# An output projection by seven block products instead of eight, for half of the tokens of a hybrid attention layer

## The chip, the cores and the metric

The kernel runs on one core of one Trainium2 chip. The metric is the device time of one execution in microseconds (us). The engines are named as the profile names them: PE multiplies matrices and PEld loads its stationary operand, DVE, ACT and POOL work on vectors, and SP issues the transfers (DMA).

## The reference

One layer of a post-norm trunk, for 1024 tokens of 1024 dimensions, in float32. The part that changes is the product with `w_out`; its result goes into the first LayerNorm.

```python
h = x @ w_in                                   # q, k, v of two kinds of attention, and two gates
y_a = chunk_band_attention(...) @ w_proj_a     # 512 x 1024 weights
y_b = stick_breaking_attention(...) @ w_proj_b
mix = (sigmoid(ga + b) * y_a + sigmoid(gb + b) * y_b) @ w_out     # 1024 x 1024 weights
x = layer_norm(2 ** 0.25 * x + mix, ln1_g, ln1_b)
g, u = split(x @ w_ffn_in, 2)                  # 1024 x 5632
x = layer_norm(2 ** 0.25 * x + (silu(g) * u) @ w_ffn_out, ln2_g, ln2_b)
```

## The kernel before

**Arithmetic.** Every operand of a matrix product is split into a high part (a cast to fp32r on ACT) and a low part (operand minus high part, by a subtraction on DVE or POOL); `split` (L109) does it. One product of two 128-row operands is then three matmuls, high by high, high by low and low by high (`mm3`, L113), each 128x128 stationary by 128x512 moving, accumulated in one PSUM bank of 512 columns.

**Seven products.** The input projection, the v projection and most of the feed-forward layer already multiply 2x2 blocks by seven block products instead of eight (a Strassen-Winograd scheme). Sums of blocks of both operands are made on DVE, split, and seven products are accumulated in two banks per output block, which are read out between the products (`pair_steps` L185, `v_steps` L446, `down_seven` L1332). The product with `w_out` is a plain one.

**Stages, in order of the text.** (1) Input projection, 14 work items one after another (`run_pairs` L508). Each item's seven products take their turn on PE while ACT and DVE read the banks into tiles `c`, split them into `hi` and `lo` and SP stores them. Beside them the weights `w_proj` are split and stored for later, one block per item from the sixth step on (`store_proj` L558, called in `aside_work` L502). (2) Attention with gates and the first branch's projection woven in. (3) The second branch's projection (loop at L1024): for each of eight blocks `c` of 128 dimensions, in the order 6, 7, 5, 4, 0, 1, 2, 3, 24 matmuls fill two banks `yBps` of 512 tokens each (two banks in turn, tag `sc`). DVE multiplies each by the gate `gB` (L1042) and adds the other branch, `gA` or `mA` (L1043); the sum, transposed `mix`, is split into `mh[c]`, `ml[c]` (L1044). (4) Output projection (L1228): first over blocks 0 to 3 for all eight token tiles, then over blocks 4 to 7. Each of the 2 x 8 x 2 groups is 12 matmuls into a bank `ops`, which DVE adds to `acc_t[tt]`, loaded with `x` (L1244). In the second round a LayerNorm follows per token tile (`layer_norm` L1056), the result is stored, and at token tile 4 the transposes that make the feed-forward layer's operands begin (`x1_operands` L1079). (5) The feed-forward layer.

**Memory.** SBUF is cut into slots of 128 x 1024 float32 with fixed counts per tag (`SLOTS` L44): `bw` 9, `pt` 4, `yt` 3, `gt` 3, `kp` 4, `op` 8, `xt` 16, and `qs`, `kh`, `kl`, `v` with 2 each. `cycle(QKV, ...)` (L69) hands out these last four tags in turn. A tile waits until a slot of its tag is free, that is, until the last reader of an earlier tile is done. The three `gt` slots hold the raw weights of `w_out` before they are split.

**Order.** The text is unrolled. The order on each engine is not the order of the text: when the program is built, a planner replays it with its own costs, and gives each queue a fixed order in which, of what is ready, the earlier in the text goes first. SP's queue is one such order, and a transfer that waits for its slot holds up those queued behind it. `keep_in_program_order` pins single instructions.

**Weights of `w_out`.** `begin_w` (L537) issues the load into a raw slot and returns `end`, which splits it: a cast on ACT (L546) and a subtraction on the engine that is passed in (L547), here DVE.

Of the kernel before, what the change touches and what calls it, by code (L numbers as in the profile page):

```python
# [12 lines left out]
F32R = mybir.dt.float32r  # L13
# [5 lines left out]
P = 128  # L19
# [11 lines left out]
HW = 512  # L31
# [17 lines left out]
def hybrid_trunk_kernel(ctx: ExitStack, tc, x, xt, w_first, w_v, w_in, b_gate, rel_bias, w_proj,  # L49
# [452 lines left out]
    def aside_work(i):  # L502
        if i == 2:
            small_inputs()
        if i >= len(work) - 9:
            store_proj(i - len(work) + 9)

# [45 lines left out]
    def load_w(*args):  # L553
        return begin_w(*args)()

# [461 lines left out]
    mh, ml = [], []  # L1017
    for c in range(8):
        m_slot = of("bw") if c < 4 else lambda name, dtype: cycle(QKV, name, dtype)
        mh.append(m_slot(f"mh{c}", F32R))  # L1020
        ml.append(m_slot(f"ml{c}", F32R))
    acc_t = [slot(tag, f"acc{tt}") for tt, tag in enumerate(["pt"] * 4 + ["yt"] * 3 + ["bw"])]
    wo_ends, wo = [], []
    for n, c in enumerate((6, 7, 5, 4, 0, 1, 2, 3)):  # L1024
# [12 lines left out]
        for hf, cs in enumerate((LO, HI)):  # L1037
# [6 lines left out]
            split(mh[c][:, cs], ml[c][:, cs], mA[:, cs])  # L1044
        if wo_ends:
            wo.append(wo_ends.pop()(True))
        if 2 < n < 7:
            wo_ends.append(begin_w(w_out[(n - 3) * P:(n - 2) * P, :], f"o0_{n - 3}", of("gt"),
                                   of("xt"), nc.vector))
# [80 lines left out]
    for tt in range(8):  # L1130
        dma(acc_t[tt], x[tt * P:(tt + 1) * P, :])
# [96 lines left out]
    for half_k in range(2):  # L1228
        if half_k == 1:
            wo = [load_w(w_out[(4 + j) * P:(5 + j) * P, :], f"o1_{j}", of("gt"), of("xt"),  # L1230
                         nc.vector) for j in range(4)]
            left_f(0)
            R0 = slot("gt", "wRf0")
            dma(R0, w_ffn_in[NF])
            Wf[0]["hr"] = split_w(R0, "wrf0", "bw")
            left_f(1)
            right_f(1)
        for tt in range(8):
            ts_ = slice(tt * P, (tt + 1) * P)
            for hf, cs in enumerate((LO, HI)):  # L1240
                acc = bank("mm" if hf == 0 else "sc", f"ops{half_k}_{tt}_{hf}")
                mm3(acc, [(mh[4 * half_k + j][:, ts_], ml[4 * half_k + j][:, ts_],
                           wo[j][0][:, cs], wo[j][1][:, cs]) for j in range(4)])
                nc.vector.scalar_tensor_tensor(  # L1244
                    acc_t[tt][:, cs], acc_t[tt][:, cs], ALPHA if half_k == 0 else 1.0, acc,
                    ALU.mult, ALU.add)
            if half_k == 1:
# [4 lines left out]
                if tt == 3:  # L1252
                    left_f(2)
# [179 lines left out]
```

## Time and profile before

| | us |
|---|---|
| median of 3 runs (lowest to highest) | 1430.65 (1429.98 to 1431.88) |
| the profiled execution's own time | 1430.51 |
| its span, first to last instruction | 1428.7 |

The granted clock of PE in the profiled execution is 0.998 of full speed. The second branch's projection lies at 641 to 685 us of the span and the output projection at 685 to 777 us; the input projection ends at 333 us. In a row of the timeline the first number is the start, the second the duration, and a bracket tells how long the engine was idle before and who ended that. In the rows of stretches each engine has its busy time and, in brackets, its instructions.

### The profile page before, as it was taken

The numbers are of one execution on the slowest core, as the hardware profiler recorded it, in microseconds if no ns is written. First come the engines' busy times: TensorE is split into PE (matmuls) and PEld (weight loads), VectorE is DVE, ScalarE is ACT, GpSimd is POOL, SyncE is SP. The second block draws the span as 40 slices with busy tenths as digits, with TensorE's granted clock in tenths as the row PEclk, the third lists the DMA queues.
The fourth block names the chain that finished last, engine by engine and source line by source line (L and its number), as shares of the span: only waits on it lengthen the run. The fifth ranks groups of instructions, "written<-read, shape, count | busy, mean of one in ns | idle before, by whom it ended". The sixth has DMA issues, their size and how long they took to land.

```text
span 1428.7 us, 19071 instructions
## 1 busy us (share of the span) xinstructions
PE 1417.4 (99%) x6696; PEld 1177.0 (82%) x6696; DVE 1027.6 (72%) x1638; ACT 672.7 (47%) x1171; POOL 267.8 (19%) x317
## 2 busy tenths in 40 slices
PE   9999999999999999999999999999999999999997
PEld 7888888888888888888888888888888888888886
DVE  8857756645778778877768947776776756978757
ACT  6434444555778887863213634443444433212201
POOL 0000000003556788740023000000000000100016
PEclk9999999999999999999999999999999999999999
DMA  7475567858786579848412124443444458797602
GB/s 251 131 235 166 191 226 216 293 189 220 212 219 187 161 212 288 262 153 309 157 45 89 62 87 150 150 157 134 148 161 162 153 187 279 281 310 238 202 15 103
DMA packets 102544, 263.99 MB, mean 185 GB/s; under 512 B 11040, under 2 KB 27424, under 8 KB 102448
## 3 DMA queue, kind: packets, MB, share of 16 engines
q1 hardware_dynamic: 102448, 262.77, 56.7%
q8 instruction: 53, 0.87, 0.3%
q14 instruction: 43, 0.35, 0.1%
HBM read 170.94 MB, written 88.11 MB: 181 GB/s over the span
## 4 chain that ended last, share of the span: by engine, by line
PE 94%; DVE 3%; ACT 1%; DMA 1%; POOL 0%; issue 0%; POOLq 0%; SPq 0%; DVEq 0%; ACTq 0%
PE sxf L180 16%; PE sxp L180 8%; PE szf L180 8%; PE dx L1356 6%; PE v L483 5%; PE gps L579 4%; PE syf L180 4%; PE szp L180 4%; PE dz L1356 3%; PE yAps L876 3%; PE syp L180 2%; PE tp_b L787 2%; PE tp_a L787 2%; PE ops L118 2%; PE ops L117 2%; PE ops L120 2%
## 5 line engine op out<-in xcount | busy, mean ns | idle before, releaser
L1312 POOL TENSOR_TENSOR wdyt<-wdyt 128x512 f32<-128x512 f32 x8 | 11.2, 1394 | 512.3 <-ACT h L1184 422.6
L764 POOL TENSOR_TENSOR w_b<-w_b,kp_b 128x511 f32<-128x511 f32 (+3 forms) x96 | 96.1, 1011 | 31.1 <-DVE kp_b L759 21.8
L759 DVE TENSOR_TENSOR_SCAN kp_b<-kp_b,ident_ps 128x512 f32<-128x512 f32 (+2 forms) x64 | 56.6, 885 | 23.6 <-ACT kp_b L756 22.7
L756 ACT ACTIVATE kp_b<-sc_b 128x512 f32<-128x512 f32 (+3 forms) x96 | 48.4, 504 | 30.7 <-PE sc_b L676 25.0
L1064 POOL TENSOR_TENSOR mv<-mv,neghalf 128x1 f32<-128x1 f32 x16 | 23.9, 1494 | 207.7 <-DVE mv L1063 207.6
L699 POOL MEMSET bias<- 64x64 f32 x2 | 0.3, 144 | 313.7 <-ACT bias L695 313.7
L180 PE MATMUL szf<-x1S63h,wcf 128*128 128x512 f32 x168 | 55.1, 389 | 0.0
L111 DVE TENSOR_TENSOR pt_b<-tp_b,pt_b 128x512 fp32r<-128x512 f32 (+1 forms) x96 | 50.0, 544 | 6.6 <-ACT pt_b L110 5.9
L729 POOL TENSOR_SCALAR w_a<-w_a,st_a 128x640 f32<-128x640 f32 (+2 forms) x64 | 42.5, 668 | 60.5 <-PE sc_a L676 24.9
L1287 DVE TENSOR_TENSOR x<-dx,x 128x512 f32<-128x512 f32 x64 | 43.3, 686 | 14.6 <-PE dx L1356 14.6
L111 DVE TENSOR_TENSOR sl<-h,sl 128x512 fp32r<-128x512 f32 x56 | 38.4, 686 | 21.0 <-ACT sl L110 21.0
L110 ACT CAST sl<-h 128x512 fp32r<-128x512 f32 x56 | 34.7, 619 | 37.5 <-PE syf L180 17.1
L110 ACT CAST pt_b<-tp_b 128x512 fp32r<-128x512 f32 (+1 forms) x96 | 47.5, 505 | 8.0 <-PE tp_b L787 7.6
L118 PE MATMUL ops<-wl_o,mh 128*128 128x512 f32 x128 | 50.1, 392 | 0.0
L724 ACT ACTIVATE w_a<-w_a,st_a 128x640 f32<-128x640 f32 (+2 forms) x64 | 44.8, 701 | 11.1 <-DVE st_a L718 9.9
L120 PE MATMUL ops<-wh_o,ml 128*128 128x512 f32 x128 | 49.9, 390 | 0.0
L117 PE MATMUL ops<-wh_o,mh 128*128 128x512 f32 x128 | 49.7, 391 | 0.0
L1184 ACT ACTIVATE h<-sxf 128x512 f32<-128x512 f32 x21 | 12.5, 598 | 77.9 <-PE sxf L180 77.9
L111 DVE TENSOR_TENSOR pt_a<-tp_a,pt_a 128x512 fp32r<-128x512 f32 (+1 forms) x96 | 44.8, 485 | 5.6 <-ACT pt_a L110 4.0
L757 ACT ACTIVATE w_b<-sc_b 128x511 f32<-128x511 f32 (+3 forms) x96 | 48.6, 506 | 0.0
L787 PE MATMUL tp_b<-ident,w_b 128*128 128x128 f32 x288 | 47.8, 273 | 0.4 <-DVE pt_b L111 0.3
L110 ACT CAST pt_a<-tp_a 128x512 fp32r<-128x512 f32 (+1 forms) x96 | 39.2, 433 | 12.4 <-PE tp_a L787 11.6
(1740 smaller groups left out, 4778.6 us busy)
## 6 DMA issues: line engine op xcount, KB each, us to landing
s_dr<-sl SPq DMA_DIRECT2D x112, 256.0 KB, 2.3
sd<-s_dr SPq DMA_DIRECT2D x56, 512.0 KB, 4.6
wLf<-in_w_ffn_in_dram SPq DMA_DIRECT2D x22, 512.0 KB, 4.4
wRf<-in_w_ffn_in_dram SPq DMA_DIRECT2D x22, 512.0 KB, 3.7
v_dr<-vc SPq DMA_DIRECT2D x16, 512.0 KB, 3.0
qs<-q_dr SPq DMA_DIRECT2D x16, 512.0 KB, 5.7
kh<-k_dr SPq DMA_DIRECT2D x32, 256.0 KB, 5.8
kl<-k_dr SPq DMA_DIRECT2D x32, 256.0 KB, 5.6
```

The lines of the kernel that those rows point to most:

```text
L110: return (nc.scalar.copy(dst_h, src), nc.vector.tensor_tensor(dst_l, src, dst_h.bitcast(F32), ALU.subtract))
L111: nc.vector.tensor_tensor(dst_l, src, dst_h.bitcast(F32), ALU.subtract))
L117: mm(acc, lh, rh, start=(i == 0), stop=False)
L118: mm(acc, lh, rl, start=False, stop=False)
L120: mm(acc, ll, rh, start=False, stop=(i == n))
L180: mm(acc, lw[:, ks], rx, start=(first and kt == i == 0), stop=(kt == 3 and i == 2), skip_group_check=not first)
L483: mm(accs[j], a, b, start=(first and kt == n == 0), stop=(kt == 3 and n == 2), skip_group_check=True)
L579: mm(acc[hf], lw[:, ks], rx[k][:, (LO, HI)[hf]], start=(k == j == 0), stop=(k == KT - 1 and j == 2))
L759: nc.vector.tensor_tensor_scan(kp[:, 0:e], kp[:, 0:e], ident_ps()[:, 0:e], 0.0, ALU.mult, ALU.add)
L764: nc.gpsimd.tensor_tensor(be[:, m0:e], be[:, m0:e], kp[:, m0 - 1:e - 1], ALU.mult)
L787: tr(tp[:, (qb - lo_q) * P:(qb - lo_q + 1) * P], wt[qb - q0][:, (kb - qb) * P:(kb - qb + 1) * P], ident)
L1356: mm(acc, a, b, start=(first and i == n == 0), stop=(i == n - 1 == 1), skip_group_check=not first)
```

## The change

`w_out` is cut in 2 x 2 blocks of 512 x 512, "11", "12", "21", "22" (the upper row of blocks being the dimensions 512 to 1023). Four combinations of them, "t1" to "t4", are computed once, in the first stage: `sum_wo` is called after the steps 5 and 8 of `run_pairs`, loads four 128 x 1024 tiles into `QKV` slots, makes four subtractions of 128 x 1024 on DVE and stores four tiles to DRAM.

In stage 3 the `mix` block of the last 512 tokens (`HI`) is split into one tile `m_high[c]`. The first 512 tokens are cut in two blocks of 256; `m_sums` makes four sums of 128 x 256 on DVE for each of the last four `c`, and splits four further operands.

In stage 4 the first 512 tokens go through seven products (order 1, 2, 6, 5, 3, 7, 4), each 2 x 4 x 3 matmuls, and the last 512 tokens through plain groups of 24 matmuls, first for the lower half of the output dimensions for all four token tiles, then for the upper half, with the LayerNorm behind each of the latter. The weights pass in the order "11", "21", "t2", "t1", "22", "t3", "t4", "12", each as two tiles of 128 x 1024. Six of the eight have their low part made on POOL, "22" and "12" on DVE. The raw tiles of the first two take `pt` slots, those of the others `gt` slots; the split ones of "11", "21", "22", "12" take `xt` slots and stay, those of "t1" to "t4" take `op` slots. The loads of `x` into `acc_t` are issued later and one by one.

```diff
+        if i in (5, 8):
+            sum_wo(i // 6)
...
+    def sum_wo(j):
+        put, sub = nc.vector.tensor_tensor, ALU.subtract
+        x_, y_, z_, u_ = (cycle(QKV, f"wo{n}r{j}") for n in ("11", "12", "21", "22"))
+        for t, n in ((x_, "11"), (y_, "12"), (u_, "22"), (z_, "21")):
+            dma(t, wo_src[n][j])
+        put(x_, y_, x_, sub)
+        put(y_, u_, y_, sub)
+        put(u_, u_, x_, sub)
+        put(z_, z_, u_, sub)
+        for t, n in ((x_, "t1"), (y_, "t3"), (u_, "t2"), (z_, "t4")):
+            dma(wt_dr[n][j], t)
...
+    def m_sums(kt, a, b):
+        put, sub = nc.vector.tensor_tensor, ALU.subtract
+        g, (q0, q1, q2, q3) = m_first[kt], (quarter(q) for q in range(4))
+        split(g[:, q2], g[:, q3], b[:, q0])
+        nc.scalar.copy(raw_22[:, quarter(kt)], b[:, q1])
+        put(b[:, q1], a[:, q1], b[:, q1], ALU.add)
+        put(a[:, q1], a[:, q0], a[:, q1], sub)
+        put(a[:, q0], b[:, q1], a[:, q0], sub)
+        put(b[:, q0], b[:, q0], a[:, q0], sub)
+        for n, t in enumerate((a, b)):
+            o = m_ab[n][kt] = slot("bw", f"m{'ab'[n]}_{kt}", F32R)
+            split(o[:, LO], o[:, HI], t[:, LO])
...
-            split(mh[c][:, cs], ml[c][:, cs], mA[:, cs])
+        m_raw[c] = mA
+        t = m_high[c] = cycle(QKV, f"mo{c}", F32R)
+        split(t[:, LO], t[:, HI], mA[:, HI])
+        if c < 4:
+            m_sums(c, m_raw[c + 4], mA)
+        else:
+            g = m_first[c - 4]
+            split(g[:, quarter(0)], g[:, quarter(1)], mA[:, quarter(0)])
+        if n in (0, 3):
+            wo_end = begin_wo(("11", "21")[n // 3], "pt", "xt", nc.gpsimd)
+        elif n in (2, 5):
+            wo_end()
+        elif n == 6:
+            more_acc("pt")
+            more_acc("pt")
+    wo_end = begin_wo("t2", "gt", "op", nc.gpsimd)
+    wo_end()
+    wo_end = begin_wo("t1", "gt", "op", nc.gpsimd)
...
+    for p in (1, 2, 6, 5, 3, 7, 4):
+        first = p in (1, 2, 5)
...
+        for j in range(2):
+            accs = by if p in (2, 5, 3) else bx
+            if first:
+                accs[j] = bank({1: "mm", 2: "sc", 5: "tr"}[p], f"ops{p}_{j}")
+            for kt in range(4):
+                lh, ll = (t[:, j * P:(j + 1) * P] for t in m_op(p, kt))
+                wh, wl = wo_op(name, kt)
+                for n, (a, b) in enumerate(((lh, wh), (lh, wl), (ll, wh))):
+                    mm(accs[j], a, b, start=(first and kt == n == 0), stop=(kt == 3 and n == 2),
+                       skip_group_check=True)
+            take_in(t0 + j, cs, accs[j], scale)
+            if p in (3, 4):
+                norm_1(t0 + j, False)
+        if p == 1:
+            wo_end()
+            wo_end = begin_wo("22", "gt", "xt", nc.vector)
+        elif p == 2:
...
+            wo_end()
+            wo_end = begin_wo("t3", "gt", "op", nc.gpsimd)
+        elif p == 6:
+            wo_end()
+            wo_end = begin_wo("t4", "gt", "op", nc.gpsimd)
+        elif p == 5:
+            wo_end()
+            wo_end = begin_wo("12", "gt", "xt", nc.vector)
...
+    for hf, cs in enumerate((LO, HI)):
+        for tt in range(4, 8):
+            acc = bank(("mm", "sc")[hf], f"ops{tt}_{hf}")
...
+            mm3(acc, pairs)          # 8 blocks of dimensions: 24 matmuls
+            take_in(tt, cs, acc)
+            if hf == 1:
+                norm_1(tt, tt > 5)
+                if tt == 4:
+                    x1_operands(0, acc_t)
```

106 lines of the change are left out of this document (67 added, 39 removed).

## The prediction

> **What bounds the kernel now.** I read the page first: the busy time by engine and the chain that ended last.
>
> ```profile
> span 1428.7 us, 19071 instructions
> PE 1417.4 (99%) x6696; PEld 1177.0 (82%) x6696; DVE 1027.6 (72%) x1638; ACT 672.7 (47%) x1171; POOL 267.8 (19%) x317
> ...
> PE 94%; DVE 3%; ACT 1%; DMA 1%; POOL 0%; issue 0%; POOLq 0%; SPq 0%; DVEq 0%; ACTq 0%
> ```
>
> PE is busy for 99% of the span and is 94% of the chain. A busy PE need not be at its peak, so the second view is what PE waited for (six rows in the whole span; the first and the last), and the third the stretches that the change touches, with the granted clock in the column after POOL.
>
> ```profile
> PE warm L267 <- DVE warm L264: 1.2, 1, 1.2
> ...
> PE x1ps L1086 <- ACT x1raw L1096: 0.2, 1, 0.2
> ```
>
> ```profile
> core 0: us, PE busy (x) PEld busy (x) DVE busy (x) ACT busy (x) POOL busy (x), PEclk, DMA share, GB/s
> 200.00:220.00 20.00, 20.00 (x90) 16.58 (x89) 10.70 (x12) 9.45 (x12) 0.00 (x0) 1.00 0.79 246
> ...
> 641.00:663.40 22.40, 22.40 (x102) 18.65 (x101) 15.85 (x24) 9.15 (x12) 0.00 (x0) 1.00 0.91 324
> 663.40:685.30 21.90, 21.90 (x98) 18.14 (x97) 18.16 (x27) 7.84 (x11) 0.00 (x0) 1.00 0.65 221
> 685.30:731.00 45.70, 45.69 (x202) 37.53 (x201) 26.55 (x35) 12.14 (x13) 0.00 (x0) 1.00 0.35 106
> 731.00:777.00 46.00, 45.82 (x217) 37.55 (x217) 40.96 (x68) 13.06 (x21) 20.09 (x11) 1.00 0.20 78
> ```
>
> PE never stands still in the input projection, in the second branch's projection (641 to 685) or in the output projection (685 to 777), at full clock. So a matmul taken out of these stages is worth its whole pitch, and every wait that the change brings in is paid in full: there is no idle PE time to hide it in. DVE is at 83% in 663.4 to 685.3 (18.16 of 21.90); that is the thin place.
>
> **What is removed.** The output projection has 2 x 8 x 2 groups of 12, 384 matmuls. Afterwards it has 7 x 24 = 168 for the first 512 tokens and 4 x 2 x 24 = 192 for the others, 360. The pitch of back-to-back ones:
>
> ```profile
> 692.06 0.39 PE L118 MATMUL ops<-wl_o,mh 128*128 128x512 f32 x1
> ...
> 692.74 0.39 PE L118 MATMUL ops<-wl_o,mh 128*128 128x512 f32 x1
> ```
>
> Every third matmul is of line 118, so the pitch is 0.68 / 3 = 0.2267 us (the 0.39 is one matmul's way through the pipeline). 24 x 0.2267 = 5.44 us go. The count follows from the loops, so that part is sure. The Trainium skill ("TensorE: Matmul & The Clock Gate", section "Wait — 56ns, not 53.3ns?") gives N / 2.4 GHz plus about 2.5 ns from start to start, which would make an estimate of 0.2157 us here and 5.18 us for the 24; the trace is 5% slower than that, and the row counts.
>
> **Stage 3, the token sums.** What DVE does now for half a block, and the nearest row for a 256-wide operation:
>
> ```profile
> 667.04 0.68 DVE L1042 TENSOR_TENSOR gB<-yBps,gB 128x512 f32<-128x512 f32 x1
> 667.76 0.69 DVE L1043 TENSOR_TENSOR mA<-gB,mA 128x512 f32<-128x512 f32 x1
> 669.14 0.69 DVE L111 TENSOR_TENSOR ml<-mA,mh 128x512 fp32r<-128x512 f32 x1 [0.69 <-ACT mh L110]
> 669.75 0.68 DVE L1042 TENSOR_TENSOR gB<-yBps,gB 128x512 f32<-128x512 f32 x1
> ```
>
> ```profile
> L111 DVE TENSOR_TENSOR pt_a<-tp_a,pt_a 128x256 fp32r<-128x256 f32 x24 | 9.9, 412 | 0.0
> ```
>
> A 256-wide one lies between half of 0.69 and this 0.41 (which reads PSUM); I take 0.38. For each of the first four blocks DVE then has L1042 and L1043 twice (2.76), one 512-wide low part (0.61, the start to start of independent ones, 669.14 to 669.75) and one 256-wide (0.38): 3.8 us beside 24 x 0.2267 = 5.44 us of PE, less than now. For each of the last four it has 2.76 + 0.61, five 256-wide (1.9) and two more 512-wide low parts (1.2): 6.5 us beside 5.44. That is 1.06 us too much per block. The cover: an L1042 is ready every 2.72 us (667.04, 669.75) and its bank is next needed 2.72 us later, so with its 0.68 it may start 2.0 us late. The first L1042 of the third such block is ready at 667.04 + 4 x 2.72 = 677.9; DVE reaches it after 2 x 6.5 us, at 680.0, 2.1 late. The later blocks have no one behind them in this stage. The bounds are nothing (the planner puts L1042 first) and 3.2 us (three excesses in full); nearest to the first, I charge 0.5. Below nothing is excluded, as PE has no idle time there to give back.
>
> **A lock between DVE and POOL.** POOL makes the low parts of twelve weight tiles. Rows from the feed-forward stage show what that does to DVE:
>
> ```profile
> 1203.45 1.45 POOL L1312 TENSOR_TENSOR wdyt<-wdyt 128x512 f32<-128x512 f32 x1 [422.57 <-ACT h L1184]
> 1203.67 1.78 DVE L1185 TENSOR_TENSOR h<-h,gt 128x512 f32<-128x512 f32 x1
> 1226.74 0.68 DVE L111 TENSOR_TENSOR wdc<-wdyt,wdc 128x512 fp32r<-128x512 f32 x1
> 1226.95 1.62 POOL L1312 TENSOR_TENSOR wdyt<-wdyt 128x512 f32<-128x512 f32 x1 [10.68 <-DVE wdgt L1311]
> 1227.34 0.68 DVE L1287 TENSOR_TENSOR x<-dx,x 128x512 f32<-128x512 f32 x1
> 1238.19 1.29 POOL L1312 TENSOR_TENSOR wdyt<-wdyt 128x512 f32<-128x512 f32 x1 [9.62 <-DVE wdgt L1311]
> 1238.62 1.41 DVE L111 TENSOR_TENSOR wdc<-wdyt,wdc 128x512 fp32r<-128x512 f32 x1
> ```
>
> A DVE operation with both inputs in SBUF that starts under a POOL one takes 1.78 or 1.41 us instead of 0.68 and ends 0.55 us after POOL's; a POOL operation that starts second takes 1.62 instead of 1.29; L1287, which reads a PSUM bank, keeps its 0.68. So one excludes the other for the length of an operation. By the Trainium skill ("SBUF — State Buffer", section "Who interferes with whom") the two share a pair of ports under an exclusive lock, taken by whoever starts first; the trace agrees (1.78 against 0.68). That speaks against this change: the sums, low parts and L1043 all read SBUF twice, and L1042 queues behind them.
>
> **Stage 4, the chain of weights.** From the third product on, raw weight tiles pass through three `gt` slots:
>
> ```profile
> L547 POOL TENSOR_TENSOR wl_g<-wr_g,wh_g 128x1024 fp32r<-128x1024 f32 x5 | 12.0, 2399 | 1.4 <-ACT wh_g L546 1.3
> L546 ACT CAST wh_o<-wr_o 128x1024 fp32r<-128x1024 f32 x8 | 8.2, 1050 | 3.7 <-DMA wr_o<-in_w_out_dram 3.7
> wr_o<-in_w_out_dram SPq DMA_DIRECT2D x8, 512.0 KB, 4.2
> ```
>
> One turn is 4.2 + 1.05 + 2.40 = 7.65 us; three slots give a pair per 5.1 us, and a product eats a pair per 5.44. It fits with 0.34 us to spare. The start: the slots are held by the kept `gA5` to `gA7`, read last by the token sums of blocks 1, 2 and 3, which end near 667.0 + 2, 3 and 4 x 6.5 = 680, 686.5 and 693. The first POOL subtraction (680 + 5.25 to 687.7) locks DVE in the middle of that, so say 680, 688.9 and 695.4. Then "t2" is complete at 688.9 + 7.65 = 696.6, while product 6 starts at 685.3 + 2 x 5.44 = 696.2 and needs the second tile's low part with its eighth matmul, at 697.8. "t1" is complete at 703.1 and needed at 703.2. I charge 1.2 us for the two together; the bounds are 0 (all as computed) and 4.8 (each meets one more POOL operation). Behind them, each of "22", "t3" and "t4" has the 0.34. The loads and the pending `acc_t` loads stand in SP's one queue, so a load that waits for its slot holds those behind it.
>
> The second half is covered: product 4 ends near 723, its `gt`, `op` and `bw` slots are free for the feed-forward weights some 50 us before their first use, and the LayerNorms follow at 24 x 0.2267 = 5.44 us each, as now, with one addition less beside each. If that cover went, the three remaining tiles would cost what they cost now, nothing.
>
> **Stage 1, the sums of weights.** Eight loads, eight stores and eight 128x1024 subtractions are added. The rows around the first call, at the end of work item 6:
>
> ```profile
> 202.65 0.59 ACT L199 COPY c<-sxp 128x512 f32<-128x512 f32 x1 [0.31 <-PE sxp L180]
> 205.17 0.39 PE L180 MATMUL sxp<-s24h,wbp7h 128*128 128x512 f32 x1
> 207.89 0.39 PE L180 MATMUL szp<-s13h,wap7h 128*128 128x512 f32 x1
> 207.90 0.34 SPq L541 DMA_DIRECT2D wr_proj<-in_w_proj_dram  x1
> L547 DVE TENSOR_TENSOR wl_proj<-wr_proj,wh_proj x8: 1217/1222/1226, 198.4 to 316.3; 128x1024 fp32r<-128x1024 f32 x8
> wp_dr<-wh_proj SPq DMA_DIRECT2D x8, 512.0 KB, 2.6
> DMA to landing us min/median/max: 3.3/4.3/7.7
> ```
>
> On DVE that is 4 x 1.22 = 4.9 us per call, beside 9.3 idle us in 200 to 220 (10.70 of 20 busy); that is covered, and without the cover it would be 9.8 us in all. The slots are not covered so surely. Counting the turns of `QKV`, the first product of work item 7 is copied (202.65) into a `qs` slot that has long been free. Afterwards the sum's first tile takes that place, and the copy has to wait until the stores of item 6's `hi` give the other `qs` slot back. In this trace the `wr_proj` load at 207.90 is the one that takes that slot, so that is when it comes free. Product 6 adds to the bank that is being copied, so it starts near 208.6 instead of 205.17, 3.4 us late. Product 5, which uses another bank and starts at 207.89 now, can go ahead of it (2.72 us), and so can the first product of the next item. The bounds are 0 (the planner has put these in) and 3.4 (it has not); I take 0.5, near the first, because the planner picks what is ready by its own time. The second call falls among the gates, which take fewer `QKV` slots; there the same count finds the slot free in time.
>
> **The sum.** 5.44 off, 0.5 on for the token sums, 1.2 for the weights, 0.5 for stage 1: 3.2 us less. Against the profiled execution's own 1430.51 that is **1427.3 us**. The median of the runs, 1430.65, lies 0.14 from that execution, so I add nothing. A measurement of this kernel can tell about 0.2%, 2.9 us, from no change.
>
> **Rivals.**
>
> *The weights eat the gain.* POOL meets a locking DVE operation, or DVE a POOL one, at both of the tight places: 4.8 us for the weights instead of 1.2. That gives 1430.51 - 5.44 + 0.5 + 4.8 + 0.5 = 1430.9, no change. For it: the reserves of 1.2 and 0.1 us that I find are smaller than one POOL operation. Against it: PE's six small waits now, in stages that are as closely packed, show that the planner's order is usually kept by the chip; and products 6 and 5 could shift only once, since a wait of one gives the next its time.
>
> *The chain of weights limits every product.* If a turn through a `gt` slot takes T, a product waits 2/3 T - 5.44. The longest landing among the loads of line 541 is 7.7 us (last row above). With it T is 11.15 and each of the five products 6, 5, 3, 7, 4 waits 2.0 us: 1430.51 - 5.44 + 0.5 + 0.5 + 10.0 = 1436.1, slower. It decides from T = 10.4 on, where the five waits of 1.46 each outweigh the 5.44 by 2.9 us together with the other two charges. For it: in 660 to 690 the `acc_t` loads, the weights and the gates share one queue, the LayerNorms of the first tokens put 2.4 us additions on POOL during products 7 and 4, and every POOL operation can be held by DVE. Against it: the DMA share in 685 to 731 is only 0.35, and landings of 4.2 are the rule there.
>
> *Stage 1 holds PE.* If the copy at 202.65 gets its slot only from the sum's first tile, that is after its load (from 207.9, 4.2), four subtractions (4.9) and a store (2.6), at 219.6, PE has work from product 5 and the next item until 210.6 and then waits 9.0 us: 1430.51 - 5.44 + 0.5 + 1.2 + 9.0 = 1435.8, slower. For it: both `qs` slots are then taken. Against it: `hi` is stored first, so its slot is the earlier one.
>
> **How the numbers follow.** Most of the gain kept, waits of at most 2.5 us: 0.48, with its own range 1425.1 (1430.51 - 5.44) to 1427.6. The weights eat the gain: 0.26. The chain limits every product: 0.18. Stage 1 holds PE: 0.08. So faster 0.48, within 0.2% 0.26, slower 0.26. The range reaches from 1424.9, a run's scatter below the whole gain, up to 1434.5, through most of the second case and into the third; about 2 in 10 are left above.
>
> **What would show it.** Right: PE's matmuls of the output projection are 360 with the same 0.227 pitch, the stretch from the last `yBps` to the first `plainhl` is 4 to 5.4 us shorter, PE's list of waits shows at most a microsecond or so on the first products' weights, and the input projection ends at 333 as now. DVE rows with two SBUF inputs under a POOL subtraction last up to 3 us. Wrong: waits of PE for `wl_o` on POOL at product after product (second rival), or for ACT's L199 near 209 (third), or a granted clock below 1.00 there, or `yBps` waiting for L1042 by more than 3 us in all.

## The result, and the profile after

The changed kernel took 1449.61 us (median of 4 runs, 1448.30 to 1450.16) against 1431.03 us (1429.98 to 1431.88) for the kernel before on the same chip: a ratio of 1.0129 (95% interval 1.0111 to 1.0146), slower by 18.6 us. The forecast was 1427.3 us, range 1424.9 to 1434.5.

The page of the profiled execution (its own time 1448.30 us): span, busy time of PE, and the chain that ended last.

```profile
span 1446.5 us, 19146 instructions
...
PE 1418.2 (98%) x6672; PEld 1173.3 (81%) x6672; DVE 1048.7 (72%) x1653; ACT 687.3 (48%) x1194; POOL 305.0 (21%) x331
...
PE 90%; DVE 3%; DMA 2%; ACT 2%; issue 1%; POOL 1%; SPq 0%; POOLq 0%; DVEq 0%; ACTq 0%
```

PE has 24 matmuls fewer (6672 against 6696), and 4% of the chain has gone from PE to engines that PE waits for. What PE waited for (total, times, longest):

```profile
PE ops L1322 <- DVE mv L1137: 7.1, 1, 7.1
PE sxp L180 <- ACT wbp9h L110: 4.9, 1, 4.9
PE yBps L117 <- DVE gB L1104: 3.0, 4, 1.2
...
PE ops L1322 <- DVE acc L1301: 0.9, 1, 0.9
```

These are three places beyond the 1.2 us at the very start, where before no wait was above 0.4 us. The stretches around them (columns as in the prediction):

```profile
core 0: us, PE busy (x) PEld busy (x) DVE busy (x) ACT busy (x) POOL busy (x), PEclk, DMA share, GB/s
...
249.00:252.00 3.00, 2.96 (x8) 1.84 (x7) 2.95 (x3) 1.32 (x2) 0.00 (x0) 0.53 0.75 248
651.10:699.00 47.90, 44.91 (x195) 35.84 (x194) 38.70 (x62) 21.38 (x33) 11.28 (x5) 1.00 0.61 220
699.00:740.00 41.00, 33.08 (x145) 26.76 (x144) 33.17 (x40) 18.64 (x21) 23.28 (x10) 0.96 0.68 229
740.00:744.00 4.00, 3.97 (x11) 3.19 (x12) 4.00 (x5) 2.17 (x2) 2.71 (x2) 0.58 0.51 157
744.00:794.90 50.90, 50.71 (x240) 41.64 (x239) 37.98 (x53) 15.98 (x24) 19.91 (x10) 1.00 0.29 104
```

The second branch's projection takes 47.9 us with PE busy for 44.9, and behind each of the two long waits the granted clock is down to 0.53 and 0.58.

I compare all kernels by four stretches of the profiled execution, between first starts of PE: from the span's start to the first `gps` (stage 1), from there to the first `yBps` (attention), to the first `ops` (stage 3), and to the first `plainhl` (stage 4). From the feed-forward layer on, before and after agree to 0.1 us. The sum of the four differences, 8.25 + 1.11 + 4.24 + 4.23, is the 17.8 us between the spans. Stage 4 should have lost 5.44, so its waits and the slow clock behind one of them cost 9.7. Attention's 1.11 us are gone in e2, which has no sums of weights (308.20); they were not followed further.

| kernel | time, us | before, us | ratio (95%) | stage 1 | attention | stage 3 | stage 4 |
|---|---|---|---|---|---|---|---|
| before | | 1430.51 (profiled) | | 333.59 | 308.21 | 43.61 | 91.65 |
| after | 1449.61 | 1431.03 | 1.0129 (1.0111 to 1.0146) | 341.84 | 309.32 | 47.85 | 95.88 |
| e1 before + weight sums | 1440.12 | 1430.53 | 1.0063 (1.0048 to 1.0078) | 341.85 | 308.69 | 43.61 | 91.63 |
| e2 after, no weight sums | 1442.31 | 1430.53 | 1.0083 (1.0068 to 1.0098) | 333.25 | 308.20 | 49.03 | 97.30 |
| e3 sums' stores on ACT's queue | 1447.83 | 1430.53 | 1.0120 (1.0104 to 1.0137) | 338.89 | 308.19 | 49.03 | 96.71 |
| e4 low part of "12" later | 1450.06 | 1430.53 | 1.0134 (1.0119 to 1.0149) | 342.54 | 308.78 | 48.53 | 96.54 |
| e5 low parts on DVE | 1442.13 | 1430.11 | 1.0083 (1.0068 to 1.0098) | 341.94 | 310.37 | 43.60 | 93.32 |
| e6 only t1 to t4 on DVE | 1447.34 | 1430.11 | 1.0120 (1.0103 to 1.0137) | 343.11 | 309.17 | 48.06 | 93.68 |
| e7 no token sums | 1445.60 | 1430.11 | 1.0110 (1.0095 to 1.0125) | 342.19 | 308.64 | 49.22 | 90.45 |
| e8 sums behind items 11, 12 | 1450.12 | 1430.11 | 1.0139 (1.0124 to 1.0154) | 333.42 | 317.11 | 49.82 | 96.25 |
| e9 sums behind items 3, 4 | 1450.76 | 1430.52 | 1.0143 (1.0129 to 1.0156) | 342.80 | 308.49 | 49.02 | 96.60 |
| e10 e5 + four banks | 1436.18 | 1430.52 | 1.0039 (1.0025 to 1.0052) | 342.23 | 308.67 | 43.87 | 87.53 |
| e11 e10 + sums as in e9 | 1436.29 | 1430.52 | 1.0039 (1.0025 to 1.0052) | 344.39 | 308.45 | 43.60 | 88.90 |
| e12 e10 + sums in four parts | 1430.89 | 1430.68 | 1.0000 (0.9991 to 1.0009) | 337.33 | 309.25 | 43.60 | 87.39 |
| e13 the parts earlier | 1437.23 | 1430.68 | 1.0047 (1.0032 to 1.0062) | 343.20 | 309.76 | 43.61 | 87.15 |
| e14 e1 without stores | 1433.73 | 1430.68 | 1.0020 (1.0010 to 1.0030) | 337.46 | 308.79 | 43.61 | 91.66 |
| e15 e1 without subtractions | 1439.18 | 1430.68 | 1.0061 (1.0046 to 1.0076) | 341.96 | 308.23 | 43.60 | 91.66 |
| e16 e12, stores on ACT's queue | 1437.59 | 1430.82 | 1.0051 (1.0038 to 1.0063) | 344.94 | 308.71 | 43.61 | 88.36 |
| e17 e10 + eight parts | 1433.20 | 1430.82 | 1.0011 (1.0002 to 1.0020) | 340.44 | 308.40 | 43.61 | 87.84 |
| e18 e12, first part last | 1431.98 | 1430.92 | 1.0007 (0.9998 to 1.0016) | 335.19 | 311.17 | 43.60 | 86.90 |

### The profile page after: what moved, and what is told of

The parts are those of the page before. It is cut to its first block, busy times and chain, and to the rows that moved or that the text cites. A ratio compares the mean times of both kernels' runs of the same rounds, so it can differ in the third digit from the quotient of the medians.

```text
span 1446.5 us, 19146 instructions
## 1 busy us (share of the span) xinstructions
PE 1418.2 (98%) x6672; PEld 1173.3 (81%) x6672; DVE 1048.7 (72%) x1653; ACT 687.3 (48%) x1194; POOL 305.0 (21%) x331
## 4 chain that ended last, share of the span: by engine, by line
PE 90%; DVE 3%; DMA 2%; ACT 2%; issue 1%; POOL 1%; SPq 0%; POOLq 0%; DVEq 0%; ACTq 0%
PE sxf L180 16%; PE sxp L180 9%; PE szf L180 8%; PE dx L1475 6%; PE v L483 5%; PE szp L180 4%; PE gps L597 4%; PE syf L180 4%; PE dz L1475 3%; PE yAps L894 3%; PE syp L180 2%; PE tp_b L805 2%; PE tp_a L805 2%; PE ops L1322 2%; PE dy L1475 2%; PE plain L349 1%
## 5 line engine op out<-in xcount | busy, mean ns | idle before, releaser
L1138 POOL TENSOR_TENSOR mv<-mv,neghalf 128x1 f32<-128x1 f32 x16 | 23.9, 1495 | 111.9 <-DVE mv L1137 111.9
L805 PEld LDWEIGHTS tp_b<-ident,w_b 128*128 128x128 f32 x288 | 35.6, 140 | 10.0 <-PE sc_b L694 1.7
L805 PE MATMUL tp_a<-ident,w_a 128*128 128x128 f32 x240 | 43.1, 275 | 0.5 <-DVE pt_a L111 0.4
L597 PE MATMUL gps<-xl,wh_g 128*128 128x512 f32 x96 | 42.9, 447 | 0.0
```

Of the source, the lines that this page charges most:

```text
L597: mm(acc[hf], lw[:, ks], rx[k][:, (LO, HI)[hf]], start=(k == j == 0), stop=(k == KT - 1 and j == 2))
L805: tr(tp[:, (qb - lo_q) * P:(qb - lo_q + 1) * P], wt[qb - q0][:, (kb - qb) * P:(kb - qb + 1) * P], ident)
```

## What the two traces show, stage by stage

**Stage 1: SP's queue.** Timeline of the kernel before, SP's issues (start, duration of the issue): the right and left weights of work items 9 and 10.

```profile
209.38 0.51 SPq L142 DMA_DIRECT2D wRp<-in_w_in_dram  x1
209.93 0.43 SPq L131 DMA_DIRECT2D wLp<-in_w_in_dram  x1
```

The same of the kernel after, shortened:

```profile
206.68 1.12 SPq L566 DMA_DIRECT2D wo11r<-in_w_out_dram  x1
...
216.22 0.33 SPq L572 DMA_DIRECT2D wt_drt<-wo11r  x1
...
221.56 0.32 SPq L572 DMA_DIRECT2D wt_drt<-wo21r  x1
...
223.89 0.45 SPq L335 DMA_DIRECT2D k_dr<-hi  x1
...
233.59 1.12 SPq L142 DMA_DIRECT2D wRp<-in_w_in_dram  x1
```

The two loads have not lost their slots; they have lost their place. The loads of the sums stand where they stood, the queue waits 6 us for the first sum, and behind the sums' stores come the stores of item 7 and of the projection's weights. The first load goes out 24 us later, and PE has nothing left (timeline of PE after):

```profile
243.16 0.39 PE L180 MATMUL syp<-xh,wlp9l 128*128 128x512 f32 x1
248.47 0.80 PE L180 MATMUL sxp<-s24h,wbp9h 128*128 128x512 f32 x1 [4.92 <-ACT wbp9h L110]
```

Counted matmul by matmul against the kernel before, PE is 5.2 us late at this restart, 7.1 us when its clock is back (see the last section) and 8.2 us by 301 us. The last 1.1 us come in small steps from 288 us on, for which the list names no wait above 0.2 us; their cause stays open.

**Stage 3: POOL's low parts.** The weights "11" arrive early, and their low parts are made on POOL among DVE's work (timeline after):

```profile
655.39 5.25 POOL L549 TENSOR_TENSOR wl_o<-wr_o,wh_o 128x1024 fp32r<-128x1024 f32 x2 [17.52 <-ACT wh_o L548]
...
658.30 0.68 DVE L1104 TENSOR_TENSOR gB<-yBps,gB 128x512 f32<-128x512 f32 x1
659.01 2.18 DVE L1105 TENSOR_TENSOR gA<-gB,gA 128x512 f32<-128x512 f32 x1
...
662.48 0.68 DVE L1104 TENSOR_TENSOR gB<-yBps,gB 128x512 f32<-128x512 f32 x1
...
663.22 0.50 PE L117 MATMUL yBps<-yh,wyh 128*128 128x512 f32 x1 [0.93 <-DVE gB L1104]
```

L1105 reads SBUF twice and takes 2.18 us under POOL's operation instead of 0.69. The L1104 that PE needs keeps its own 0.68 but stands behind it in DVE's queue. Three of the four waits, at 663.22, 672.14 and 676.31 us, are ahead of the first token sum at 682.78. The list counts a wait from the end of the matmul before; with the restarts of PE its 3.0 us come to the 4.24 by which the stretch is longer, at a clock of 1.00.

**Stage 4: POOL's queue.** The stop of PE ahead of product 4, from 732.58 to 740.03, in the timeline after:

```profile
722.54 10.48 POOL L549 TENSOR_TENSOR wl_ot<-wr_ot,wh_ot 128x1024 fp32r<-128x1024 f32 x4 [7.33 <-ACT wh_ot L548]
...
726.54 0.15 DVE L1137 TENSOR_SCALAR mv<-mv 128x1 f32<-128x1 f32 x1
...
727.33 3.69 SPq L543 DMA_DIRECT2D wr_o<-in_w_out_dram  x2
...
732.99 1.55 POOL L1138 TENSOR_TENSOR mv<-mv,neghalf 128x1 f32<-128x1 f32 x1
...
734.57 1.15 ACT L1146 ACTIVATE acc<-acc,mv 128x1024 f32<-128x1024 f32 x1 [2.54 <-POOL mv L1138]
735.62 1.03 ACT L548 CAST wh_o<-wr_o 128x1024 fp32r<-128x1024 f32 x1
...
736.68 2.54 DVE L549 TENSOR_TENSOR wl_o<-wr_o,wh_o 128x1024 fp32r<-128x1024 f32 x1 [1.97 <-ACT wh_o L548]
...
739.26 0.63 DVE L1301 SCALAR_TENSOR_TENSOR acc<-acc,ops 128x512 f32<-128x512 f32 x1
...
740.03 0.77 PE L1322 MATMUL ops<-wh_ot,m22h 128*128 128x512 f32 x1 [7.06 <-DVE mv L1137]
```

Read from the top: the first LayerNorm has its variance at 726.7, but its power (L1138, the variance to the power of -1/2) is on POOL behind four low parts of "t3" and "t4" and starts at 733.0. ACT waits for it and makes the second high part of "12" only afterwards, DVE waits for that, and behind DVE's low part (2.54 us instead of 1.21, under POOL's addition for the same LayerNorm from 735.79 on) stands the take-in of product 7 that clears the bank of product 4. A second path from the same four low parts ends at nearly the same time: SP issues the second load of "12" at 730.69, when POOL's third low part (over at 730.66) gives its `gt` slot back, and the trace has it landed at 734.36, while the power ends at 734.53. Without the power ACT could have begun that high part some 1.3 us sooner, no more. The list of waits names L1137, a neighbour of the take-in in DVE's queue; the root is five steps up. These rows leave one doubt: DVE's order, with the low parts of "12" ahead of the take-in, may be enough by itself. That is what e4 asked.

## The experiments

Each is an edit of the kernel before or of the changed kernel. All times stand in the table above.

**e1, e2: stage 1 by itself, and the rest by itself.** e1 adds `sum_wo` and its calls to the kernel before; e2 drops the calls and reads `wo_src` for "t1" to "t4".

> The kernel before, with the sums of the projection's weights added to its first stage exactly as in the changed kernel (same loads, sums and stores, same work items); nothing reads them, and the output projection is that of before. Theory (SP's queue): the sums' loads and stores stand in SP's queue ahead of the loads of the weights of work item 9, and nothing else of the change is needed for the loss of stage 1: the input projection ends, by the first product of the gates, at 341 to 342 instead of 333.6, PE waits once for about 5 us for the right sums of item 9, and the run takes 1438 to 1440 us. Rival (the loss of stage 1 is made up later, because attention has slack): 1430 to 1432 us.

> The changed kernel without the sums of the first stage: the seven products read four blocks of the projection's weights in the places of the four sums, so the output of the first 512 tokens is not the reference's; every load, split and matmul of the stages after the first is there. Theory (SP's queue): stage 1 is as before (gates begin at 333.6), and 8 to 9.5 us go: 1440 to 1441.6 us. What is left above the kernel before, 9 to 11 us, is the loss of the stages of the mixing and of the output projection. Rival (the stages after are late because stage 1 is late and their loads bunch): with stage 1 on time they lose nothing either, and the run comes out near 1425.6, the forecast of the matmuls alone.

The sums alone cost the kernel before 9.6 us, with the same wait of 4.9 us at the same place; nothing later gave it back. Without them the changed kernel is 7.3 us faster, and its stages 3 and 4 lose more than before (49.0 and 97.3; in stage 3 the clock now falls to half behind a stop of 2.68 us). So there are separate causes, and a late stage 1 is not the reason for the later ones.

**e3: the stores of the sums on ACT's queue.**

```diff
-            dma(wt_dr[n][j], t)
+            nc.scalar.dma_start(wt_dr[n][j], t)
```

> The changed kernel with the eight stores of the weights' sums issued from ScalarE's queue instead of SyncE's; loads, sums, slots and the work on VectorE stay. Theory (SP's queue): with those waiting stores gone the loads of item 9's weights go out some 20 us earlier, PE's wait of 5.3 us at item 9 and the slow clock behind it go, and the gates begin at 334 to 336: 1441 to 1443.5 us. Rival (VectorE's sums or the slots they take are the cause): the wait at item 9 stays at 4 us or more and the time within 2 us of 1449.6.

The time missed the expectation by 4 us; the mechanism was half right. The load of item 9's weights goes out at 210.3 instead of 233.6 and its wait is gone, so the queue was the reason for that wait. But stage 1 is only 2.95 us shorter: SP now waits elsewhere, up to 9.7 us at a time, for slots that the sums' stores hold (waits of SP, 200 to 300 us):

```profile
SPq L543 <- DMA wt_drt<-wo11r: 11.3, 2, 9.7
```

**e4: high and low part of "12" pinned behind the take-in of product 7.**

```diff
         elif p == 7:
-            wo_end()
+            wo_end(True)      # both instructions of each tile: keep_in_program_order
```

> The changed kernel with one thing reordered: the high and low parts of weight block 12 are queued on ScalarE and VectorE behind the take-in of product 7 instead of ahead of it. Theory (VectorE's queue): PE's wait of 7.45 us ahead of product 4 shrinks to under 1 us, what is left being GpSimd's low parts of t4, which end at 733.0, and the slower clock of the 4 us behind it goes as well: 1440.5 to 1442.5 us. Rival (GpSimd's lock or the layer norms hold the take-in of product 7 in any order): the wait stays above 4 us and the time is 1446 to 1450.

DVE's order around this one take-in is not enough as a cause. Product 4 no longer waits, but the first tile of the second half does, with a stop of 6.87 us (timeline of e4):

```profile
723.11 11.46 POOL L549 TENSOR_TENSOR wl_ot<-wr_ot,wh_ot 128x1024 fp32r<-128x1024 f32 x4 [7.04 <-ACT wh_ot L548]
...
734.53 0.57 POOL L1138 TENSOR_TENSOR mv<-mv,neghalf 128x1 f32<-128x1 f32 x1
...
735.13 1.15 ACT L1146 ACTIVATE acc<-acc,mv 128x1024 f32<-128x1024 f32 x1 [4.91 <-POOL mv L1138]
...
741.41 3.67 DVE L549 TENSOR_TENSOR wl_o<-wr_o,wh_o 128x1024 fp32r<-128x1024 f32 x2 [6.87 <-ACT wh_o L548]
```

The same chain from POOL's four low parts, through two LayerNorms and one take-in further on. So the next edit took away its head.

**e5, e6: the low parts on DVE.** `nc.gpsimd` becomes `nc.vector` in the calls of `begin_wo`: in e5 all, in e6 only those of "t1" to "t4".

> The changed kernel with the twelve low parts of the projection's weights (11, 21, t2, t1, t3, t4) on VectorE instead of GpSimd. Theory (GpSimd's low parts are the cause behind the first stage: each holds VectorE's operations for about 2 us, and four in a row hold the power of the layer norm for 10.5 us, behind which stand ScalarE's high parts of block 12, VectorE's low parts and the take-in that product 4 needs): the yB stage falls from 47.9 to 44.5 us or less, the wait of 7.45 us ahead of product 4 and that of 1.3 ahead of product 3 go under 1 us together, and the run takes 1435 to 1439 us. Rival (VectorE is simply full there: 14.5 us more of work, 12 by 1.21, at the same place): the yB stage takes 48 us or more, product 6 waits as well, and the time is 1448 to 1455.

> The changed kernel with only the eight low parts of the sums (t2, t1, t3, t4) on VectorE; the four of blocks 11 and 21, made early in the yB stage, stay on GpSimd. Theory (GpSimd's low parts): the two first waits of the yB stage, 1.3 and 1.5 to 2.8 us, which stand behind the low parts of 11 and 21, stay; the later ones of the yB stage and the wait ahead of product 4 go: 1438 to 1441.5 us, 2 to 3.5 above the kernel with all twelve moved. Rival (VectorE full): 1448 or more.

With all twelve on DVE stage 3 is back at 43.60 us. The row of this stretch in e5, columns as above:

```profile
652.30:695.90 43.60, 43.60 (x194) 36.10 (x194) 38.83 (x67) 21.51 (x34) 0.00 (x0) 1.00 0.67 241
```

DVE does the four low parts of "11" and "21" in addition (4 x 1.21 us) and is busy for 38.83 us, as in the changed kernel (38.70), which had let POOL do them: the lock had cost as much as the work. The waits at product 4 are down to 0.2 and 0.7 us. (The planner has also put one low part of "12" behind the take-in here, so e5 moves the head of the chain and this order together.) The time, 1442.1, missed the expected 1435 to 1439, mostly because a wait of 4.1 us appeared ahead of the second half's third tile: the take-in that clears its bank stood on DVE behind sums for the first feed-forward weights. One of these met the lock again, under POOL's addition of a LayerNorm (timeline of e5):

```profile
746.57 2.48 POOL L1147 TENSOR_TENSOR acc<-acc,ln1b 128x1024 f32<-128x1024 f32 x1 [1.26 <-ACT acc L1146]
...
746.77 2.83 DVE L159 TENSOR_TENSOR taf<-wRf 128x512 f32<-128x512 f32 x1
```

e6 missed by more: the later waits of stage 3 stayed too. They go only when the low parts of "11" and "21" are moved too, so I take them for a backlog of the first ones; moving "t1" to "t4" gains 2.2 us in stage 4 and nothing in stage 3.

**e7: without the four sums per block in `m_sums`.**

> The changed kernel without the four sums of tokens in each of the last four blocks of the mixing (16 operations of 128x256 on VectorE, which the prediction put at 0.5 us); splits, copies, loads and matmuls stay, so the output of the first 512 tokens is not the reference's. Theory (GpSimd's low parts): the waits stay nearly all, the yB stage is 46 to 48 us and the wait ahead of product 4 is 7 us: 1446.5 to 1449.6. Rival (the sums overfill VectorE, as the prediction had it, only more so): the yB stage falls to 44 us and the time to 1444 to 1446.

Stage 3 keeps its waits (49.2), so the token sums are not its cause, as the theory says. But the rival's time came out, from another place: stage 4 gained 5.4 us. Without the sums POOL's low parts of "t3" and "t4" end at 726.4, and the first power does not queue behind them (timeline of e7):

```profile
729.27 1.55 POOL L1134 TENSOR_TENSOR mv<-mv,neghalf 128x1 f32<-128x1 f32 x1 [2.92 <-DVE mv L1133]
```

PE's longest wait in stage 4 is then 1.1 us, with the low parts still on POOL. So it matters when POOL makes them, and not only that it does. (The take-in of product 7 stands ahead of the second low part of "12" here too.) The sums are the last readers of the tiles that hold the `gt` slots, which would explain the earlier weights; this was not tried apart.

**e8, e9: the weight sums behind other work items.**

```diff
-        if i in (5, 8):
-            sum_wo(i // 6)
+        if i in (10, 11):          # e9: (2, 3)
+            sum_wo(i - 10)
```

> The changed kernel with the weights' sums made behind work items 11 and 12 instead of 6 and 9, where one load of weights of the first stage is left behind them in SyncE's queue instead of eight. Theory (SP's queue): PE's wait of 5.3 us at item 9 goes, and the gates begin at 334 to 337 instead of 341.8, less if the last load, of item 13, comes late; the time is 1441.5 to 1445. Rival (the first stage has no room for the 4 MB and the sums anywhere, or the loss moves to the start of attention): attention ends by 8 us later than in the kernel before all the same, and the time is 1448 to 1450.

> The changed kernel with the weights' sums made behind work items 3 and 4 instead of 6 and 9: ahead of the V projection, where the DMA share of the kernel before is 0.73, 0.53 and 0.32 in the slices of 20 us from 100 to 160 us, and where no re-layout of the projections stands in the queue. Theory (what the first stage lost is the place of the sums in SyncE's queue and in the slots from item 6 on, not their work): no wait at item 9, gates begin at 333.5 to 335, attention loses nothing, and the time is 1440.5 to 1442.5. Rival (4 MB in, 4 MB out and eight sums cost their 8 us wherever they stand, as they did behind items 11 and 12, where attention lost 8.7): the gates or the V projection come some 8 us late, 1448 to 1450.

Both rivals held, with times just above their ranges. Behind items 11 and 12 stage 1 is as before (333.4) and attention loses 8.9 us, its first scores waiting; the stretch of e8 there, with a DMA share of 1.07 (over 1, as the view counts a packet whole in the stretch where it starts):

```profile
340.00:350.00 10.00, 7.38 (x32) 5.10 (x30) 2.93 (x11) 4.35 (x7) 0.29 (x2) 0.99 1.07 285
```

Behind items 3 and 4 the V projection waits instead, once for 5.2 us (PE's waits in e9):

```profile
PE v L483 <- ACT vc L493: 5.2, 1, 5.2
```

Wherever the sums stood as two lumps, attention ended 8.7 to 11.0 us later than before.

**e10, e11: four banks in the second half; and all edits together.**

```diff
-            acc = bank(("mm", "sc")[hf], f"ops{tt}_{hf}")
+            acc = bank(("sc", "mm")[tt % 2], f"ops{tt}_{hf}")
```

> The changed kernel with the twelve low parts on VectorE and, in the second half's first pass, the four accumulators in four banks (two of each tag in turn) instead of two. Theory (what was left in the output projection with the low parts on VectorE is one take-in queued behind the first feed-forward weights, which a bank more would hide): the wait of 4.25 us ahead of the second half's third tile and the slower clock behind it go, 5 to 5.5 us from the 1442.1 with the low parts alone: 1436.5 to 1437.5. Rival (VectorE is late as a whole there, and a bank more only moves the wait to a later tile): 1440 to 1442.

> The changed kernel with the three edits together: sums behind items 3 and 4, low parts on VectorE, four banks. Theory (three causes that add up): 8 to 8.3 us less than with the low parts and banks alone, 1428 to 1429.5, which is 0.5 to 2 us below the kernel before at 1430.1. Rival (they don't add up: stages after an early first stage lose again): 1431 to 1437.

e10 comes out 0.3 us below its range, as the theory has it: 6.0 us less than e5, no wait at the third tile, and stage 4 takes 87.53 us. That is 4.1 less than before; of the 5.44 of the matmuls 1.3 are lost to small waits. e11 missed: the early sums bring nothing (1436.29 against 1436.18). Its stretches are from an execution 3.3 us above its median.

**e12 to e18: what of the sums costs the time.** All but e14 and e15 build on e10. e12 and e13 cut them in four parts with two slots each, e17 in eight with one slot; e14 and e15 are e1 without the stores and without the subtractions; e16 and e18 vary e12.

```diff
+    def sum_wo(n):                 # e12: steps (3, 6, 8, 10), e13: (2, 3, 7, 9), e18: (6, 8, 10, 11)
+        j, cs = n // 2, (LO, HI)[n % 2]
+        a, b = (cycle(QKV, f"wo{s}r{n}") for s in "ab")
+        x_, y_, u_, z_ = a[:, LO], a[:, HI], b[:, LO], b[:, HI]
...                                 # loads, sums and stores of 128 x 512
```

> The changed kernel with the low parts on VectorE and the four banks, and its weights' sums cut into four equal parts (1 MB in, 1 MB out, two slots each) behind work items 4, 7, 9 and 11 instead of two (2 MB in, 2 MB out, four slots each) behind 6 and 9. Theory (the first stage loses because one lump holds four of eight slots and SyncE's queue at one place; each item has room for a smaller one): no wait of PE over 2 us in the first stage, gates at 334 to 336.5, and the time 1428.5 to 1431 against 1436.2 with the two lumps. Rival (the 8 MB and the sums cost their 8 us in any parts): gates at 340 or later, 1435 to 1437.

> As the run before, the four parts behind work items 3, 4, 8 and 10. Theory (lumps): the same, gates at 334 to 336.5, 1428.5 to 1431; the two parts ahead of the V projection hold its slots, so up to 2 us may be lost there. Rival (any parts cost the same): 1435 to 1437.

> The kernel before with the sums' loads and the sums themselves in the first stage, as in the run that took 1440.1, but without their eight stores; nothing reads the sums. Theory (the stores hold the slots and SyncE's queue until the sums are made and written): half to most of the 9.6 us go, 1431 to 1435. Rival (the loads and VectorE's eight sums are the cost): 1438 to 1440.

> The kernel before with the sums' loads and stores but without the eight subtractions between them: the blocks are copied, and nothing reads them. Theory (queue and slots): the stores wait for their loads alone and SyncE passes them sooner, but slots and queue are still held for the transfers: 1433 to 1439. Rival (VectorE's eight sums and the waits for them are the whole cost): 1430.5 to 1432.

> The run with four parts behind work items 4, 7, 9 and 11, with their stores issued from ScalarE's queue. Theory (what is left of the first stage's loss, 3.7 us at the gates, is the stores in SyncE's queue ahead of the weights' loads): the gates begin at 334 to 336 instead of 337.3, and the time is 1428 to 1430, up to 0.2% below the kernel before. Rival (what is left is the slots and the transfers themselves, which no queue changes): 1430 to 1432.

> The same sums in eight parts of half the size, one slot each, behind work items 4 and 6 to 12, with the stores on SyncE's queue. Theory (lumps): smaller ones are hidden better, gates at 334 to 336, 1428 to 1430. Rival (eight places in the queue instead of four, each with eight issues, hold up one load of weights each, and pieces of 1 KB a row move slower): gates at 338 to 342, 1431 to 1436.

> As the run with four parts (1430.9, level with the kernel before), with the first part moved from behind work item 4, where it cost the V projection's weights 0.4 us of wait, to behind item 12. Theory (each item from 7 on has room for one part): the gates begin at 335 to 336.5 instead of 337.3, attention loses no more than the 1.1 us it lost there, and the time is 1429 to 1430.5. Rival (the part behind item 12 stands ahead of attention's first q and k loads, as both lumps did in the run behind 11 and 12): the gates come earlier by 1 to 2 us, and attention gives back 1 to 4: 1430 to 1434.

The times of e12 and e14 came inside their ranges (e12 with the gates at 337.3, later than expected), e15 came 0.2 us above its own. e13, e17 and e18 went with their rivals, and e16 lies 5.6 us above both of its ranges.

The subtractions cost nothing that can be told apart (e15 and e1: overlapping intervals). But PE's long wait is another one without them: 5.5 us at item 11 instead of 4.9 at item 9. So the second call can be the one that costs, and the parts of this loss do not add up one by one. The stores are most of it: without them 6.5 of the 9.6 us go (e14). In parts the same bytes cost stage 1 3.7 us instead of 8.6 (e12 against e10), if none of the parts but one stands ahead of the V projection (e13 loses 9.6). But neither taking the stores off SP's queue nor smaller parts helps further. In e16 the ACT copy L199 waits for a slot that a sum's tile holds until its store has landed (waits of ACT in e16, 225 to 260 us):

```profile
ACT c L199 <- DMA wt_drt<-wobr: 9.0, 1, 9.0
```

PE then waits 3.8 us for this copy. It is the wait on L199 that the prediction had as its third rival, in another kernel. In e17 the same copy waits 11.6 us, there for a store of q, and PE 4.0. e18 brings stage 1 down to 335.2 and attention gives 1.9 of it back.

The best version, e12, is level with the kernel before: stage 4 wins 4.3 us, stage 1 and attention lose 3.7 and 1.0. No version tried is faster than the kernel before. If the gains of e2 and e10 add up, the change with sums that cost nothing would be faster than the kernel before by an estimated 1.6 us (from the medians) to 3.9 us (from the stretches of e10: 4.12 won in stage 4, 0.26 lost in stage 3); that was not run, and whether a place without cost exists stays open.

## Why the prediction was wrong

**The matmuls: right.** They are 360, at the same pitch; with all but 0.7 us of the waits gone stage 4 takes 86.9 us in e18, where 91.65 - 5.44 is 86.2.

**Stage 3, the token sums: the wrong term.** I charged 0.5 us for the sums and nothing for the lock. The sums cost nothing in this stage (e5 has them all and takes 43.60; twice 0.68 + 0.69 is 2.74, not the 2.76 of the sum, which changes nothing), and the 4.24 us came from the low parts of "11" and "21" on POOL. The prediction had measured the lock (1.78 us instead of 0.68) and said that L1042 queues behind such an operation. The step that failed is that it then gave the lock a price at the weights of stage 4 only. In the trace after, L1105 takes 2.18 and 2.16 us under the two pairs of low parts. The sign that I had named for this stage, `yBps` waiting for L1042 by more than 3 us in all, came out at 3.0.

**Stage 4, the chain of weights: right suspect, wrong path.** The charge was 1.2 us, for PE waiting on a low part, and there was no such wait; the waits cost 9.7 us. The step that failed is that behind "t1" it gave "22", "t3" and "t4" the 0.34 us to spare and put products 3, 7 and 4 at nothing, as if PE could wait for a weight tile alone. What PE waited for was a bank: its take-in stood on DVE behind a low part of "12", this behind a high part on ACT, and this behind the load of "12" and the LayerNorm's power, which both came after four low parts on POOL (10.48 us). I had these LayerNorms only in the second rival, as additions that hold up the weights. "The second half is covered" held in this kernel (no wait above 0.2 us from 744 us on) and failed in e5, where the take-in of the third tile was late. The token sums do cost here what they do not in stage 3: without them stage 4 gains 5.4 us (e7). The rival of the chain (1436.1) had slower right, and the turn through the `gt` slots was late as it says; but PE stopped once, for the bank of product 4, and not at every product for its weights.

**Stage 1: the wrong queue.** I followed one copy to its slot. That part came as forecast: the copy moved from 202.65 to 207.76 and the planner put product 5 ahead, without a wait. But the charge of 0.5 us left out SP's queue, where two loads of weights lost their place to the sums and came 24 to 25 us later. Nor is the queue all of the 8.25 us: where it was cleared, the slots and the stores that hold them took its place (e3, e16). The idle time of DVE did cover the subtractions, as I had it (e15), but it was never they that cost the time. For the second call too I counted slots and not the queue; the 1.1 us that PE loses in small steps around it are not explained.

**A wait is paid in full: too little.** Behind the long waits of stages 1 and 4 PE ran at half clock for some microseconds, about 1.7 us more each (below). Together that makes 3.4 of the 17.8 us.

The runs also corrected theories formed after the result: DVE's order in stage 4 (e4), "t1" to "t4" as the cause of stage 3's later waits (e6), and SP's queue as the whole cause of stage 1 (e3, e8, e9).

## What to carry to other kernels

For every step that is moved or added, list the queue of each engine and of SP at that place with what stands behind it, not only the engine's free time: here a small power on POOL, a take-in on DVE and two loads on SP were late, each behind work that itself had room. Work given to POOL to relieve DVE may cost DVE the same again, if DVE's operations read SBUF twice. A temporary that goes out to DRAM holds its slot until the store has landed; here four parts cost less than two lumps, and eight no less than four.

## What the runs showed of the hardware

**The clock after a stop.** Rows of PE alone (busy, clock, DMA share, GB/s), after the stop of 7.45 us in the changed kernel:

```profile
740.00:741.00 1.00, 0.97 (x2) 0.50 0.89 176
...
742.00:743.00 1.00, 1.00 (x4) 0.50 0.16 62
743.00:744.00 1.00, 1.00 (x5) 0.83 0.00 0
744.00:745.00 1.00, 1.00 (x6) 1.00 0.59 61
```

The clock is half for 3.3 us, and the matmuls start 0.43 us apart (once 0.56) instead of 0.23, so some 1.7 us are lost beyond the wait. (The x counts every matmul that overlaps a row.) The stops of 5.31 us (at 243) and of 4.48 us (e5, at 746) show the same 0.50; in e17 it lasts 5.2 us after one of 4.38. All 20 stops of 4.1 us or more in these traces, from start to start of two matmuls, were followed by 0.50. Between 2.6 and 2.9 us the length does not decide. In e3 a matmul that started 2.67 us after the one before it still ran at 1.00 (first row), and so did those behind 2.86 us in e4 and 2.85 in e7; but behind a stop of 2.64 us in the same run e3, over at 669.88, the clock fell to 0.50 (second row), and so it did behind 2.68 us in e2. What decides there is not shown.

```profile
285.40:287.00 1.60, 0.86 (x3) 1.00 0.58 213
...
670.70:674.00 3.30, 3.30 (x9) 0.50 0.52 159
```

The Trainium skill ("TensorE: Matmul & The Clock Gate", section "HAM oscillation — how this bites in real kernels") says that a wait for data which crosses the activity window sets PE back to half rate, so that the next work starts cold. The traces agree, with 0.50 after every stop of 4.1 us and more.

**The lock lets a PSUM reader pass.** L1104, with one input in PSUM, takes 0.68 us under the POOL operation that stretches L1105 to 2.18. The Trainium skill ("SBUF — State Buffer", section "Who interferes with whom") says that a DVE instruction with at most one SBUF input, outside the 2-port perf modes, does not contend with GpSimd; the trace agrees, with these 0.68 us.
